# The last seven-product block's second group, product by product, with two token tiles normed and stored ahead of the others

## The chip, the cores and the metric

The kernel runs on one core of one Trainium2 chip. The metric is device microseconds for one execution. Names of engines as in the profile: PE is TensorE (PEld its weight loads), DVE is VectorE, ACT is ScalarE, POOL is GpSimd, SP is SyncE, which here issues DMAs.

## The reference

One layer of a decoder block over 512 tokens of width 2048. Cut to what the change touches:

```python
def _hybrid_layer(h, ...):
    u = _rmsnorm(h, norm_w)
    proj = jnp.matmul(u, w_in)                       # 2048 x 20528
    ...
    y_a = jnp.matmul(h_a, w_out[:ML_WIDTH])          # first 2048 rows of w_out
    y_b = jnp.matmul(h_b, w_out[ML_WIDTH:])          # last 2048 rows
    return jax.nn.sigmoid(gate_a) * y_a + jax.nn.sigmoid(gate_b) * y_b

def reference(x, ...):
    h = x + _hybrid_layer(x, ...)
    return _rmsnorm(h, final_norm_w)                 # over the 2048 columns of each token
```

All is float32. The change lies in the last step: the product `h_b` by the last 2048 rows of `w_out`, its gate, the sum with everything else, and the final norm.

## The kernel before, in words

**Precision.** Each float32 operand of a product is split into a high part (an ACT cast, `split_hi`, L135) and the rest (a DVE subtraction, `split_lo`, L138). One product of 128 rows by 512 columns is then three matmuls: high by high, rest by high, high by rest (L589 to L591).

**Token tiles.** The 512 tokens are four tiles of 128 (NC = 4): 0 and 1 are the lower half, 2 and 3 the upper.

**A seven-product block.** `seven_stage` (L499) computes 512 tokens by 1024 columns in blocks. Tokens, columns (`c1` and `c2`, NO = 512 each) and the 2048 rows of the weights are halved each, and eight half-size products become seven, at the price of sums of weights and of operands beforehand. A block has two groups, A with four products (m6, m1, m5, m7) and B with three (m1, m5, m7), each over KH = 8 "quads" of two 128-row weight tiles. For a quad, `load_quad` (L507) issues three 256 KB loads on SP into a buffer `wr3` (three of these); `prep_sums` and `prep_pair` make the weight sums on DVE (`t13`, `ts`) and split them. In group A, `ts` is w22 − w12 + w11 (of the four weight tiles w11, w12, w21, w22 by rows and columns): it is split, and also written to DRAM (`t2o_d`, on the ACT queue, L545), and group B reads it back and subtracts it from w21 (L549), which gives t4. Group B's products of a quad stand next to each other on PE: w21, w22, t4 with the operands `uh`/`ul` and `t4h`/`t4l`. The last six products of a block are in an order of their own (L610).

**The sums.** When a product has had its last quad, `ends` adds it up: U1 and C22 in the tile `X2`, m1 and m5 in PSUM (`add`, L637). In group B the sink takes over.

**The last stage.** OUTS has two blocks, columns 0 to 1023 and 1024 to 2047. Their sink is `sink_y` (L1328). It loads the gate tiles (`ty`, from `tg_d`, L1335, into the four 256 KB buffers tagged "wr") and multiplies: (gate + 1) by the sum (`put`, L1340). For the first block the result is added into `y_d` in DRAM by an accumulating DMA on POOL's queue (L1342). For the last block `y_d` has been loaded into the tile `hf`, 4 tiles by 2048 columns (`load_hf`, L1302, begun at the last block's group B by `open_hf`, L1320), the product is added to it on DVE (L1346), and ACT squares it with a running sum into `ssf` (L1347). The first 1024 columns are squared (L1316) and multiplied by the norm's weights `fw` on POOL (L1317) meanwhile.

**The end.** When all blocks are done, a loop over the four token tiles (L1441) makes each factor (a sum and a scale on DVE, a power on POOL), multiplies the first 1024 columns on ACT (L1446), the rest on DVE (L1449, L1452), and stores each half, 512 KB, on SP (L1447, L1453).

**What precedes.** The last 512-column block of the product by the first half of `w_out` is done plainly: 16 weight tiles, each for four token tiles, then four evictions on DVE (L1432), then the seven-product blocks begin. `h_sums` and the split of `h_b` (L1208, L1209) run beside it.

**Order.** PE's order is the program's. On the other engines a scheduler places instructions by priority: `tc.high_priority` and `urgent(n)` move them ahead, `behind(e)` puts one directly after the newest split on that engine. `start(generator, n)` runs a piece of side work n ticks later, a tick being about one product. Every engine and every DMA queue runs its own list in order: an instruction that waits holds those behind it.

Of the kernel before, what the change touches and what calls it, by code (L numbers as in the profile page):

```python
# [32 lines left out]
KLAST = 4  # L33
QWAIT = 9
# [21 lines left out]
def hybrid_body(  # L56
# [442 lines left out]
    def seven_stage(sbp, su, s4, X, t2_d, w_, k0, blocks, sinks, hook, by_half=False):  # L499
# [4 lines left out]
        quads = [(kind, c1, c2, b, g, i) for b, (kind, c1, c2) in enumerate(blocks) for g in "AB" for i in range(KH)]  # L504
        rawq, partq = [], {}
# [25 lines left out]
        def prep_sums(q):  # L531
# [5 lines left out]
            with tc.high_priority(offset=2 * PRIO):  # L537
                ts = wp.tile([P, 1, NO], F32, tag="tg", name="ts", bufs=3)
                if g == "A":
# [5 lines left out]
                    nc.scalar.dma_start(t2_d[b % 2, i], ts[:, 0, :])  # L545
# [30 lines left out]
        def seven(n0, kind, c1, c2):  # L576
# [4 lines left out]
                    "B": sinks[kind](c1, c2, m1, m5, m7, n0 + 2 * KH == len(quads))}  # L581

            def product(n, m, ts=range(2)):
# [3 lines left out]
                for t in ts:  # L587
# [7 lines left out]

            N = 2 * KH
            for n in range(N - 2):
                hook(n0 + n)
# [11 lines left out]
            for n, m in ((N - 2, 0), (N - 2, 1), (N - 1, 0), (N - 1, 1), (N - 2, 2), (N - 1, 2)):  # L610
# [5 lines left out]
                if last and m == 2 and by_half:  # L616

                    if n == N - 2:
                        for t in range(2):
                            product(N - 2, 2, (t,))  # L620
                            product(N - 1, 2, (t,))
                    continue
                if last and (n, m) == (N - 1, 1):
                    hook(len(quads) - 1)
# [118 lines left out]
    def begin_mixers(q):  # L743

        if q == 2 * KH * len(SEVEN) - 1:
            limit[0] = len(plan)
            prepare(nfront - 1)
# [511 lines left out]
    def close():  # L1259
        if "sb" not in late and not active:  # L1260
# [4 lines left out]
            late["ssf"] = sb.tile([P, NC, 3], F32, tag="ssf", name="ssf")  # L1265
            late["rf"] = sb.tile([P, NC], F32, tag="rf", name="rf")
# [30 lines left out]
    X2, ssf = late["X"], late["ssf"]  # L1297
    OUTS = [("y", c, c + NO) for c in range(0, D, 2 * NO)]
    hp = {}

    def load_hf():

        hf, fw = hp["hf"], hp["fw"]
        for i in range(4):
            nc.sync.dma_start(fw[:, i * NO:(i + 1) * NO], final_norm_w[i * NO:(i + 1) * NO].partition_broadcast(P))
            yield 1
        for c in (2, 3, 0, 1):
            nc.sync.dma_start(hf[:, c, HD:D], y_d[c, :, HD:D])
            yield 2
        for c in range(NC):  # L1310
            nc.sync.dma_start(hf[:, c, 0:HD], y_d[c, :, 0:HD])
            yield 2
        for c in range(NC):
            jk = hp["pool"].tile([P, HD], F32, tag="jk", name="jkf")
            with behind("A"):
                A.activation(jk, hf[:, c, 0:HD], AF.Square, accum_out=ssf[:, c, 0:1])  # L1316
            G.tensor_tensor(out=hf[:, c, 0:HD], in0=hf[:, c, 0:HD], in1=fw[:, 0:HD], op=ALU.mult)  # L1317
            yield 2

    def open_hf(q):  # L1320
        if q == 2 * KH * (len(OUTS) - 1) + KH:
            h2s.close()
            hp["pool"] = h2s.enter_context(tc.tile_pool(name="hfp", bufs=1))
            hp["hf"] = hp["pool"].tile([P, NC, D], F32, tag="hf", name="hf")
            hp["fw"] = hp["pool"].tile([P, D], F32, tag="fw", name="fw")
            start(load_hf(), 2)

    def sink_y(c1, c2, m1, m5, m7, last):  # L1328
# [8 lines left out]
        def put(key, ps, c, col, now=True):  # L1337
# [3 lines left out]
            if not last:  # L1341
                G.dma_start(y_d[c, :, col:col + NO], t, accum_op=ALU.add)  # L1342
                return
            o = hp["hf"][:, c, col:col + NO]
            with urgent(3) if now else behind("V"):
                V.tensor_tensor(out=o, in0=o, in1=t, op=ALU.add)  # L1346
            A.activation(t, o, AF.Square, accum_out=ssf[:, c, 1 + (col - c1) // NO:2 + (col - c1) // NO])  # L1347
# [6 lines left out]
        def half_b():  # L1354
# [5 lines left out]
            yield 2  # L1360
            if last:
                for t in range(2):
                    w = tgs[21, t] = hp["pool"].tile([P, NO], F32, tag=f"ty{t}", name="ty")
                    nc.sync.dma_start(w, tg_d[2 + t, :, D + c1:D + c1 + NO])
            yield 9 if last else 5
            for t in range(2):
                put((22, t), C22[t], 2 + t, c2, now=False)
                if last:
                    G.tensor_tensor(out=hp["hf"][:, 2 + t, c2:c2 + NO], in0=hp["hf"][:, 2 + t, c2:c2 + NO],
                                    in1=hp["fw"][:, c2:c2 + NO], op=ALU.mult)  # L1370
                yield 1
            yield 2 if last else 5
# [4 lines left out]
        def end7(t):  # L1377
            add(U1[t], U1[t], m7[t])
            if last:
                put((21, t), U1[t], 2 + t, c1)  # L1380
            else:
                start(late_((21, t), 2 + t, c1, U1[t]), 8 + 2 * t)
# [5 lines left out]
        start(half_b(), 4 * KH + 2)  # L1388
        return (lambda t: put((11, t), m1[t], t, c1)), end5, end7

    lead, seven = seven_stage(late["sb"], late["su"], late["s4"], X2, t2o_d, w_out, KT, OUTS, {"y": sink_y}, open_hf, True)
# [3 lines left out]
    for nb in range(YNARROW * NB // NO, D // NO):  # L1395
# [25 lines left out]
        for kt in range(KT):  # L1421
            hi, lo = next_w("o", nb * NO, kt)
# [61 lines left out]
```

## Time and profile before

| | us |
|---|---|
| median of three runs | 2243.85 (2242.92 to 2244.1) |
| profiled execution | 2241.4 |
| its span, first to last instruction | 2239.6 |
| mean granted clock | 0.993 |
| PE busy | 2174.5 (97%) |
| DVE, ACT, POOL busy | 1651.8, 944.0, 276.9 |

Times within the profile are in microseconds from the start of the span. A timeline row has the start, the length, the engine, the line, the operation, the tiles written and read, and in brackets how long the engine stood before it and what released it. A row of windows gives the length of a stretch and each engine's busy time in it. "SPq" and "POOLq" are instructions that issue DMAs.

### The profile page before, as it was taken

The numbers are of one execution on the slowest core, as the hardware profiler recorded it, in microseconds if no ns is written. First come the engines' busy times: TensorE is split into PE (matmuls) and PEld (weight loads), VectorE is DVE, ScalarE is ACT, GpSimd is POOL, SyncE is SP. The second block draws the span as 40 slices with busy tenths as digits, with TensorE's granted clock in tenths as the row PEclk, the third lists the DMA queues.
The fourth block names the chain that finished last, engine by engine and source line by source line (L and its number), as shares of the span: only waits on it lengthen the run. The fifth ranks groups of instructions, "written<-read, shape, count | busy, mean of one in ns | idle before, by whom it ended". The sixth has DMA issues, their size and how long they took to land.

```text
span 2239.6 us, 33118 instructions
## 1 busy us (share of the span) xinstructions
PE 2174.5 (97%) x11408; PEld 1817.6 (81%) x11408; DVE 1651.8 (74%) x2915; ACT 944.0 (42%) x1816; POOL 276.9 (12%) x342
## 2 busy tenths in 40 slices
PE   7999999999999999999999999999999999999995
PEld 5987878788778878887888888888888899987774
DVE  5787788788778777847877677776767774646786
ACT  4444444445444443443434344434434344333434
POOL 0320000000000000002322231313222110000003
PEclk9999999999999999999999999999999999999998
DMA  5456666667667766867676666667575566847686
GB/s 160 126 167 197 203 196 214 194 202 230 204 208 225 241 206 199 257 184 188 154 166 152 148 163 142 164 140 175 132 170 138 139 170 184 266 156 250 211 249 236
DMA packets 540203, 420.16 MB, mean 188 GB/s; under 512 B 241282, under 2 KB 417635, under 8 KB 540035
## 3 DMA queue, kind: packets, MB, share of 16 engines
q1 hardware_dynamic: 441986, 356.11, 56.7%
q10 hardware_dynamic: 96896, 59.86, 8.7%
q0 software_dynamic: 1152, 2.10, 0.6%
q8 instruction: 89, 1.46, 0.3%
q14 instruction: 80, 0.65, 0.1%
HBM read 332.93 MB, written 85.00 MB: 187 GB/s over the span
## 4 chain that ended last, share of the span: by engine, by line
PE 63%; DMA 16%; DVE 11%; issue 4%; SPq 3%; ACT 2%; POOL 0%; DVEq 0%; ACTq 0%; POOLq 0%
PE pj L257 9%; PE pj L259 9%; PE pj L258 9%; PE ps L590 8%; PE ps L589 8%; PE ps L591 8%; DVE wl L138 5%; DMA wr<-t_d 4%; DMA wr<-in_w_in_dram 3%; DMA wr<-t2o_d 2%; SPq L519 1%; PE pjt L272 1%; PE pjt L274 1%; PE pjt L275 1%; DMA hr<-h_d 1%
## 5 line engine op out<-in xcount | busy, mean ns | idle before, releaser
L135 ACT CAST wh<-wr 128x512 fp32r<-128x512 f32 (+1 forms) x560 | 390.1, 698 | 545.3 <-PE pj L258 290.0
L138 DVE TENSOR_TENSOR wl<-wr,wh 128x512 fp32r<-128x512 f32 (+1 forms) x560 | 462.9, 829 | 176.0 <-ACT wh L135 169.9
L257 PE MATMUL pj<-uh,wh 128*128 128x512 f32 x1024 | 429.6, 420 | 4.4 <-ACT yp L801 4.4
L259 PE MATMUL pj<-uh,wl 128*128 128x512 f32 x1024 | 401.4, 392 | 0.0
L258 PE MATMUL pj<-ul,wh 128*128 128x512 f32 x1024 | 400.4, 391 | 0.0
L589 PE MATMUL ps<-wh,uh 128*128 128x512 f32 x624 | 245.2, 393 | 8.1 <-DVE X L639 4.9
L590 PE MATMUL ps<-wl,uh 128*128 128x512 f32 x624 | 246.4, 395 | 5.0 <-DVE wl L138 4.7
L591 PE MATMUL ps<-wh,ul 128*128 128x512 f32 x624 | 243.6, 390 | 0.0
L259 PEld LDWEIGHTS pj<-uh,wl 128*128 128x128 f32 x1024 | 192.8, 188 | 43.3
L257 PEld LDWEIGHTS pj<-uh,wh 128*128 128x128 f32 x1024 | 193.8, 189 | 39.4 <-ACT yp L801 4.8
L135 ACT CAST wh<-ts 128x512 fp32r<-128x512 f32 x208 | 128.3, 617 | 228.2 <-DVE ts L549 180.2
L258 PEld LDWEIGHTS pj<-ul,wh 128*128 128x128 f32 x1024 | 193.8, 189 | 33.1
L135 ACT CAST wh<-t 128x1024 fp32r<-128x1024 f32 x104 | 109.5, 1053 | 232.9 <-PE ps L591 137.8
L590 PE MATMUL ps<-wl,suh 128*128 128x512 f32 x528 | 205.6, 389 | 0.5 <-DVE wl L138 0.5
L589 PE MATMUL ps<-wh,suh 128*128 128x512 f32 x528 | 205.7, 390 | 0.3 <-ACT to L650 0.2
L591 PE MATMUL ps<-wh,sul 128*128 128x512 f32 x528 | 205.4, 389 | 0.0
L138 DVE TENSOR_TENSOR wl<-ts,wh 128x512 fp32r<-128x512 f32 x208 | 144.9, 700 | 31.5 <-ACT wh L135 31.5
L138 DVE TENSOR_TENSOR wl<-t,wh 128x1024 fp32r<-128x1024 f32 x104 | 127.3, 1224 | 45.8 <-ACT wh L135 45.3
L589 PEld LDWEIGHTS ps<-wh,uh 128*128 128x128 f32 x624 | 117.1, 188 | 39.9 <-DVE X L639 12.0
L590 PEld LDWEIGHTS ps<-wl,uh 128*128 128x128 f32 x624 | 117.1, 188 | 38.2 <-DVE wl L138 15.3
L272 PE MATMUL pjt<-wh,uh 128*128 128x256 f32 x512 | 147.4, 288 | 0.7 <-ACT tgs L757 0.7
L274 PE MATMUL pjt<-wl,uh 128*128 128x256 f32 x512 | 144.7, 283 | 0.0
(307 smaller groups left out, 3812.9 us busy)
## 6 DMA issues: line engine op xcount, KB each, us to landing
wr<-in_w_in_dram SPq DMA_DIRECT2D x680, 256.0 KB, 3.7
wr<-in_w_out_dram SPq DMA_DIRECT2D x144, 256.0 KB, 4.5
t_d<-ts ACTq DMA_DIRECT2D x88, 256.0 KB, 4.4
wr<-t_d SPq DMA_DIRECT2D x88, 256.0 KB, 4.0
wr<-in_w_in_dram SPq DMA_DIRECT2D x96, 128.0 KB, 3.1
xt<-in_x_dram SPq DMA_DIRECT2D x8, 512.0 KB, 7.9
v<-v_d SPq DMA_DIRECT2D x8, 512.0 KB, 6.2
gb<-rows_d SPq DMA_DIRECT2D x16, 256.0 KB, 5.0
```

What stands on the lines that cost most here:

```text
L135: newest["A"] = A.copy(hi, src).ins
L138: newest["V"] = V.tensor_tensor(out=lo, in0=src, in1=hi.bitcast(F32), op=ALU.subtract).ins
L257: T.matmul(ps[j], hi[:, k, wsl], uh[:, kt, :], start=(kt == 0), stop=False)
L258: T.matmul(ps[j], hi[:, k, wsl], ul[:, kt, :], start=False, stop=False)
L259: T.matmul(ps[j], lo[:, k, wsl], uh[:, kt, :], start=False, stop=(kt == KT - 1))
L272: T.matmul(o, uh[:, kt, tsl], hi[:, k, :], start=(kt == 0 and c % 2 == 0), stop=False, skip_group_check=True)
L274: T.matmul(o, uh[:, kt, tsl], lo[:, k, :], start=False, stop=False, skip_group_check=True)
L275: T.matmul(o, ul[:, kt, tsl], hi[:, k, :], start=False, stop=(kt == KT - 1), skip_group_check=True)
L519: nc.sync.dma_start(r[:, n, :], src[n])
L589: T.matmul(ps[t], ah, hi, start=(g == "A" and i == 0), stop=False, skip_group_check=True)
L590: T.matmul(ps[t], ah, lo, start=False, stop=False, skip_group_check=True)
L591: T.matmul(ps[t], al, hi, start=False, stop=(i == KH - 1), skip_group_check=True)
```

## The change

In the last of the two output blocks:

- **Group A.** For each quad a further tile `b21` (w21, 256 KB) is loaded on SP into a "wr" buffer. POOL subtracts `ts` from it, which gives t4, and its own queue stores t4 where `ts` went before (`t2o_d`). The ACT queue's store is gone there.
- **Group B** no longer goes quad by quad but product by product: eight pieces of m5 (w22), eight of m7 (t4, read back ready), eight of m1 (w21). A piece is one 256 KB load on SP into a "wr" buffer, one cast, one split, and the six matmuls of the product's two token tiles. Loads run four pieces ahead, splits two to three.
- **Side work** is given by hand, piece by piece, in the table `beside`: loads of `y_d` in twelve parts, of the weights in two, the gate products, sums and squares. Additions for `c2` and six multiplications by weights are on POOL.
- **The last four pieces** (KLAST) are done for token tile 0 first, then for 1. Ahead of them in the program stand the factor products and the stores of tiles 2 and 3, whose sums are complete after m7.
- All eight gate tiles are loaded late in group A, into the `wr3` buffers.

Elsewhere:

- **KTAIL.** In the last plain block, the last two weight tiles are done token tile by token tile, with each tile's eviction directly behind it. The evictions of both plain 512-column blocks are at `urgent(3)` instead of `urgent()`.
- **Addresses.** `ssf` and `rf`, 64 bytes a partition together, move from the pool `sb2` into the tile `bia`. The tiles `t13` and `w2h`, `w2l` (and the operands `tuh`, `tul`) begin at a multiple of 512 bytes in a partition thereby; they began 96 bytes past one.
- The hooks `open_hf` and `begin_mixers` are simplified and `by_half` is gone.

```diff
+                    if in_final(b):
+                        G.tensor_tensor(out=b21[q], in0=b21[q], in1=ts[:, 0, :], op=ALU.subtract)
+                        G.dma_start(t2_d[b % 2, i], b21[q])
+                        load_b21(q + 1)
+                    else:
+                        nc.scalar.dma_start(t2_d[b % 2, i], ts[:, 0, :])
...
+                b21[q] = wp.tile([P, NO], F32, tag="wr", name="b21", bufs=NRAW)
+                nc.sync.dma_start(b21[q], w_[k2, c1:c1 + NO])
...
+                for m in range(4):
+                    for n in (KH - 2, KH - 1):
+                        fin(2 * m + n - KH + 2)
+                        product(n, m)
+                fin(8)
+                return
...
-            late["ssf"] = sb.tile([P, NC, 3], F32, tag="ssf", name="ssf")
-            late["rf"] = sb.tile([P, NC], F32, tag="rf", name="rf")
...
+    ssf, rf = bia[:, 0:3 * NC].rearrange("p (c n) -> p c n", c=NC), bia[:, 3 * NC:4 * NC]
...
+    def final_y(c1, c2, m1, m5, m7, lhs, split, t4_d):
...
+        pieces = [(m, i) for m in (1, 2, 0) for i in range(KH)]
...
+        def load_gates():
+            order = ((2, c2), (3, c2), (0, c2), (1, c2), (2, c1), (3, c1), (0, c1), (1, c1))
+            for n, (c, col) in enumerate(order):
+                if n % 3 == 0:
+                    t = late["sb"].tile([P, 3, NO], F32, tag="wr3", name="ty", bufs=3)
+                o = ty[c, col] = t[:, n % 3, :]
+                nc.sync.dma_start(o, tg_d[c, :, D + col:D + col + NO])
+                yield 1
+        def load():
+            if len(rawp) < len(pieces):
+                m, i = pieces[len(rawp)]
+                k2 = slice((KT + 2 * i + 1) * P, (KT + 2 * i + 2) * P)
+                with tc.high_priority(offset=2 * PRIO):
+                    r = wp.tile([P, 1, NO], F32, tag="wr", name="wr", bufs=NRAW)
+                    newest["S"] = nc.sync.dma_start(r[:, 0, :], (w_out[k2, c1:c1 + NO], w_out[k2, c2:c2 + NO], t4_d[i])[m]).ins
+                rawp.append(r)
+        def prep():
+            if len(partp) < len(pieces):
+                with tc.high_priority(offset=2 * PRIO):
+                    partp.append(split(rawp[len(partp)], False)[0])
...
+        beside = {
+            0: [lambda: known(2, c2, D)], 1: [lambda: known(3, c2, D)], 2: [lambda: known(0, c2, D)],
+            3: [lambda: known(1, c2, D), lambda: times(2, c2, C22[0])],
+            4: [lambda: known(2, c1, c2), lambda: times(3, c2, C22[1]), lambda: plus(2, c2, G)],
+            5: [lambda: known(3, c1, c2), lambda: plus(3, c2, G)],
+            6: [lambda: weight(0, HD), lambda: square(2, c2, D, 2)],
+            7: [lambda: square(3, c2, D, 2)],
+            8: [lambda: known(2, 0, HD), lambda: add(m5[0], U1[0], m5[0])],
+            9: [lambda: add(m5[1], U1[1], m5[1]), lambda: times(0, c2, m5[0])],
+            10: [lambda: known(3, 0, HD), lambda: times(1, c2, m5[1]), lambda: plus(0, c2, G)],
+            11: [lambda: plus(1, c2, G), lambda: square(2, 0, HD, 0), lambda: weigh(2, 0, HD)],
+            12: [lambda: weight(HD, D)],
+            13: [lambda: square(3, 0, HD, 0), lambda: weigh(3, 0, HD), lambda: known(0, 0, HD)],
+            14: [lambda: square(0, c2, D, 2)],
+            15: [lambda: square(1, c2, D, 2), lambda: weigh(0, c2, D), lambda: known(1, 0, HD)],
+            16: [lambda: weigh(1, c2, D), lambda: add(U1[0], U1[0], m7[0]), lambda: times(2, c1, U1[0], False), lambda: plus(2, c1, V, False),
+                 lambda: square(2, c1, c2, 1), lambda: known(0, c1, c2), lambda: known(1, c1, c2)],
+            17: [lambda: add(U1[1], U1[1], m7[1]), lambda: times(3, c1, U1[1], False), lambda: plus(3, c1, V, False),
+                 lambda: square(3, c1, c2, 1), lambda: factor(2), lambda: square(0, 0, HD, 0), lambda: weigh(0, 0, HD)],
+            18: [lambda: factor(3), lambda: square(1, 0, HD, 0), lambda: weigh(1, 0, HD)],
+        }
...
+            for t in range(2):
+                for j in range(len(pieces) - KLAST, len(pieces)):
+                    if t == 0 and j < len(pieces) - KLAST + 2:
+                        c = 2 + j - len(pieces) + KLAST
+                        by_act(c, 0, HD)
+                        store(c, 0, HD)
+                        by_dve(c, HD, D)
+                        store(c, HD, D)
+                    part(j, t)
+                times(t, c1, m1[t], False)
+                plus(t, c1, V, False)
+                square(t, c1, c2, 1, False)
+                factor(t, False)
+                by_act(t, 0, HD, False)
+                store(t, 0, HD)
+                by_dve(t, c1, c2, False)
+                by_dve(t, c2, D, False, True)
+                store(t, HD, D)
...
+        tail = KTAIL if nb == D // NO - 1 else 0
...
+        ws = [next_w("o", nb * NO, kt) for kt in range(KT - tail, KT)]
         for c in range(NC):
-            with urgent():
+            for i, w in enumerate(ws):
+                products(KT - tail + i, c, *w)
+                if i % 2:
+                    tick()
+            with urgent(3):
                 V.scalar_tensor_tensor(out=tgs[c], in0=tgs[c], scalar=1.0, in1=ps[c], op0=ALU.add, op1=ALU.mult)
```

Of the helpers in it, `known` loads a part of `y_d` into `hf` and `weight` a part of `fw`; `times` is the gate product on DVE, `plus` the addition into `hf`, `square` ACT's square with its sum, `weigh` the product with `fw` on POOL, `factor` the reduction, scale and power, `by_act` and `by_dve` the two halves of the last product, `store` the output DMA. Those not marked `False` are issued right behind the newest split of their engine.

More of the change, by code (lines that the diff above doesn't have):

```diff
@@ L33 @@
 KLAST = 4
+KTAIL = 2
 QWAIT = 9
@@ L615, in seven @@
                     load_quad()
[L616 to L622, printed above, removed]
                 if last and (n, m) == (N - 1, 1):
-                    hook(len(quads) - 1)
+                    hook()
                 product(n, m)
@@ L1296, in hybrid_body @@
     t2o_d = dr.tile([2, KH, P, NO], F32, tag="t2o", name="t2o_d")
-    X2, ssf = late["X"], late["ssf"]
+    X2 = late["X"]
     OUTS = [("y", c, c + NO) for c in range(0, D, 2 * NO)]
[L1299 to L1326, printed above, removed]
+    ssf, rf = bia[:, 0:3 * NC].rearrange("p (c n) -> p c n", c=NC), bia[:, 3 * NC:4 * NC]
     def sink_y(c1, c2, m1, m5, m7, last):
@@ L1340, in put @@
                 V.scalar_tensor_tensor(out=t, in0=t, scalar=1.0, in1=ps, op0=ALU.add, op1=ALU.mult)
[L1341 to L1347, printed above, removed]
+            G.dma_start(y_d[c, :, col:col + NO], t, accum_op=ALU.add)
         def late_(n, c, col, x_):
@@ L1378, in end7 @@
             add(U1[t], U1[t], m7[t])
[L1379 to L1382, printed above, removed]
+            start(late_((21, t), 2 + t, c1, U1[t]), 8 + 2 * t)
         def end5(t):
@@ L1437, in hybrid_body @@
         seven(2 * KH * b, *blk)
[L1438 to L1453 removed]
+    assert not active
 def hybrid_block(tc, *args):
```

167 lines of the change are left out of this document (121 added, 46 removed).

## The prediction

> **What bounds the kernel now.** I read the page's whole-span figures first, then busy time by five-microsecond windows over the end, then the timeline there.
>
> ```profile
> PE 2174.5 (97%) x11408; PEld 1817.6 (81%) x11408; DVE 1651.8 (74%) x2915; ACT 944.0 (42%) x1816; POOL 276.9 (12%) x342
> ```
> ```profile
> 2130.00:2180.00 50.00, 49.24 (x212) 39.15 (x210) 41.31 (x53) 18.11 (x26) 5.19 (x6) 1.00 0.87 247
> ```
> ```profile
> 2190.00:2195.00 5.00, 5.00 (x23) 4.00 (x23) 1.76 (x3) 1.61 (x2) 0.00 (x0) 1.00 1.05 395
> ...
> 2210.00:2215.00 5.00, 5.00 (x23) 4.04 (x23) 5.00 (x4) 2.53 (x6) 5.00 (x3) 1.00 0.00 0
> ```
>
> In each window row the busy times of PE, PEld, DVE, ACT and POOL follow its length; the last three figures are the clock, the DMA share and GB/s. TensorE is the bound for 97% of the span. In the last block's first group (row 2130:2180) VectorE is busy 41.3 of 50 us, so it has 8.7 to spare. In the second group the DMA engines are full (395 GB/s at 2190), then empty (0 at 2210). The output leaves when all else is over:
>
> ```profile
> 2215.15 0.39 PE L591 MATMUL ps<-wh,ul 128*128 128x512 f32 x1
> ...
> 2224.57 0.61 ACT L1347 ACTIVATE ty<-hf 128x512 f32<-128x512 f32 x1
> ...
> 2224.78 3.55 POOL L1445 TENSOR_TENSOR rf<-rf,mhalf 128x1 f32<-128x1 f32 x4 [4.71 <-DVE rf L1443]
> 2225.09 0.19 ACT L1347 ACTIVATION_READ_ACCUMULATOR ty<-hf 128x1 f32 x1
> 2225.31 0.16 DVE L1442 TENSOR_REDUCE rf<-ssf 128x1 f32<-128x3 f32 x1 [0.27 <-ACT ty L1347]
> 2225.39 4.27 ACT L1446 ACTIVATE hf<-hf,rf 128x1024 f32<-128x1024 f32 x4
> ...
> 2226.56 0.34 SPq L1447 DMA_DIRECT2D out_dram<-hf  x1
> ...
> 2233.28 1.19 SPq L1453 DMA_DIRECT2D out_dram<-hf  x1
> ```
> ```profile
> wr<-in_w_out_dram SPq DMA_DIRECT2D x30, 256.0 KB, 5.8
> hf<-y_d SPq DMA_DIRECT2D x8, 512.0 KB, 7.6
> out_dram<-hf SPq DMA_DIRECT2D x8, 512.0 KB, 4.9
> ...
> y_d<-ty POOLq DMA_DIRECT2D x6, 256.0 KB, 7.4
> ```
>
> The last matmul ends at about 2215.4 (its row starts at 2215.15 and is drawn 0.39 long; starts are 0.23 apart). The span ends at 2239.6. So 24.2 us are tail: eight stores of 512 KB from 2226.56 to 2233.28, the last landing 4.9 us after its issue is over.
>
> **The tail: minus 13.** The two upper token tiles (2 and 3) have their factors and stores before the last pieces end. Behind the last matmul only tile 1 is left: gate product, addition (0.68 each, as the 128x512 VectorE rows below), square and its read (0.61 and 0.19), reduce (0.16) and scale (as much, two instructions of 128x1), power (3.55/4 = 0.89), ScalarE product (4.27/4 = 1.07), issue (0.34 alone, 1.19 when queued), landing 4.9. The sum is 9.7 to 10.5; tile 0's two stores share the wire with tile 1's, so I take 11. Tail 24.2 − 11 = 13.2 gained; 12 to 14.5 as ends.
>
> **Group B by pieces: plus 5.5.** Eight quads of three loads and three products become 24 pieces of one 256 KB load and one product each, in the order m5, m7, m1; a piece is 6 matmuls, 6 × 0.23 = 1.38 us. The eight sums t4 leave VectorE here. Each needs one cast, one residual split and one load, and both rings (raw, split) hold four. A buffer's round is landing + cast 0.61 (as a 128x512 ScalarE row) + split 0.68; four pieces of PE are 5.5 us. So a landing of 4.2 us is free, and each microsecond above it costs one per round, some five rounds in 24 pieces after the ring's first filling.
>
> ```profile
> hf<-y_d SPq DMA_DIRECT2D x3, 512.0 KB, 7.4
> wr<-in_w_out_dram SPq DMA_DIRECT2D x4, 256.0 KB, 7.1
> ```
> ```profile
> DMA packets 2659, 4.85 MB, mean 243 GB/s; under 512 B 297, under 2 KB 297, under 8 KB 2658
> ...
> wr<-in_w_out_dram SPq DMA_DIRECT2D x8, 256.0 KB, 4.7
> ```
>
> The first fence is window 2180 to 2190 (350 GB/s), the second 2160 to 2180. At 243 GB/s a piece lands in 4.7; beside a flood of hf loads in 7.1. Group B keeps its bytes: 24 pieces (6.3 MB), hf (8 × 512 KB = 4.2 MB), weights 1.0 MB: 11.5 MB over 33 us is 348 GB/s, but hf now comes one load every one to three pieces instead of in a flood. I take 4.9: five rounds of 0.7 are 3.5. Ends: 4.4 (+1) and 6.5 (+11.5).
>
> ```profile
> 2194.43 0.95 SPq L519 DMA_DIRECT2D wr<-in_w_out_dram  x2
> ```
>
> SP issues 24 pieces, 12 hf loads (8 before) and two of weights (4 before) in this stretch: 38 × 0.48 = 18 us of 33, so its queue holds, as long as no load at its head waits.
>
> ```profile
> 2207.02 0.68 DVE L138 TENSOR_TENSOR wl<-ts,wh 128x512 fp32r<-128x512 f32 x1
> ...
> 2209.36 2.90 DVE L138 TENSOR_TENSOR wl<-ts,wh 128x512 fp32r<-128x512 f32 x1
> 2212.19 1.27 DVE L1340 SCALAR_TENSOR_TENSOR ty<-ty,ps 128x512 f32<-128x512 f32 x2
> ```
> ```profile
> 2202.17 2.54 POOL L1369 TENSOR_TENSOR hf<-hf,fw 128x512 f32<-128x512 f32 x2 [45.11 <-DMA wr<-in_w_out_dram]
> 2208.74 11.33 POOL L1317 TENSOR_TENSOR hf<-hf,fw 128x1024 f32<-128x1024 f32 x4 [4.04 <-ACT jkf L1316]
> ```
>
> The same split takes 0.68 and, begun while GpSimd multiplies hf by the weights (11.33/4 = 2.83 each), 2.90: it waits until GpSimd's instruction ends. Before, those four fell where no split was due; now four of 2.83 and six of 1.27 (two weight products, four additions) lie between pieces 4 and 18, beside splits on which the next load depends. One hit costs up to 2.2 us; the split ring runs up to two pieces ahead, 2.8 us, while landings are on time. I add 2 (ends 0 and 5).
>
> By the Trainium skill's "SBUF — State Buffer" (Who interferes with whom), the loser of the shared port blocks for the whole instruction of whoever issued first; the trace agrees (2.90 against 0.68). What that would make of the time is the third rival.
>
> **Group A with t4 computed on GpSimd: plus 6.** Eight GpSimd subtractions (1.27 each), eight GpSimd-queue stores in place of eight ScalarE ones, and eight more 256 KB loads, which take their buffers from the four "wr" that the ty tiles use.
>
> ```profile
> PE ps L590 <- DVE wl L138: 1.6, 4, 0.6
> PE ps L589 <- DVE X L639: 0.8, 1, 0.8
> ```
> ```profile
> 2126.25 0.69 DVE L543 TENSOR_TENSOR ts<-wr,t 128x512 f32<-128x512 f32 x1
> ...
> 2135.66 0.68 DVE L1340 SCALAR_TENSOR_TENSOR ty<-ty,ps 128x512 f32<-128x512 f32 x1
> ...
> 2136.63 0.86 POOL L1342 DMA_DIRECT2D y_d<-ty  x1 [0.94 <-DVE ty L1340]
> ...
> 2138.61 5.25 SPq L1335 DMA_DIRECT2D ty<-tg_d  x4
> ```
> ```profile
> 2143.95 14.29 SPq L519 DMA_DIRECT2D wr<-in_w_out_dram  x12
> ```
>
> The fourth ty tile of the block before now takes the buffer of the first t4. That one is free only when its subtraction (behind the ts of quad 0 that ends at 2126.94, plus 1.27) and its store have landed: 0.86 of issue, then 4.9 (the out row) to 7.4 (the y_d row), so 2134 to 2136.5; then the ty load, 4.9 more: 2139 to 2141. The gate product that ran at 2135.66 waits for it. Queued behind it on VectorE are the U1 sum and quad A1's splits, for which TensorE waits from about 2137.5: 1.5 to 3.5, I take 2.5. SP stands likewise before the 2138.61 group, whose later tiles need the y_d landings, so that the quads' loads of 2143.95 slip 3 to 4; the three-deep ring leaves 1 of it at quad 4 and 2.5 at quad 7. Together 6 (ends 2 and 10). VectorE's spare 8.7 covers eight port hits of up to 1.27; without it they cost up to 10.
>
> Before's own waits in this block are 2.4 by the waits view (1.6 + 0.8), some 3.2 from start to start, since the matmul ahead of a wait is drawn with its length. They go: the 0.8 for X because group B now begins with m5, which reads no sum, the 1.6 because the new waits above take their place. So minus 3.2.
>
> **KTAIL: minus 1.5.**
>
> ```profile
> 2051.28 0.40 PE L591 MATMUL ps<-wh,tul 128*128 128x512 f32 x1
> ...
> 2053.60 0.68 DVE L1432 SCALAR_TENSOR_TENSOR X<-X,py 128x512 f32<-128x512 f32 x1
> ...
> 2054.43 0.47 PE L589 MATMUL ps<-wh,uh 128*128 128x512 f32 x1 [2.75 <-DVE X L1432]
> ```
> ```profile
> 2055.00:2059.00 4.00, 4.00 (x12) 3.15 (x11) 4.00 (x7) 0.69 (x2) 0.00 (x0) 0.57 0.82 285
> ```
>
> TensorE stands 2.75 for the eviction at 2053.60, and runs four microseconds at clock 0.57, which costs 4 × 0.43 = 1.7. The eviction of tile 0 may now start 4 us sooner, but stays behind the same splits on VectorE, and the last weight tile's split is needed some 1.5 earlier. Between 0 and 4.5 I take 1.5.
>
> "TensorE: Matmul & The Clock Gate" (Part 1: The HAM clock gate) in the Trainium skill has the clock halve after some 3.4 us of idle; the trace shows it after 2.75 with short gaps before. By either, a group-A wait of 3.5 would cost 1.7 more, and my 2.5 none.
>
> **Operands at 512 bytes: minus 2.**
>
> ```profile
> L589 PE MATMUL ps<-wh,suh x240: 389/389/499, 518.2 to 874.0; 128*128 128x512 f32 x120
> ```
> ```profile
> L589 PE MATMUL ps<-wh,tuh x90: 387/394/400, 2060.2 to 2178.2; 128*128 128x512 f32 x90
> ```
>
> The accumulators ssf and rf, moved out of the pool, take the 96 bytes out of the addresses behind them; the move itself issues nothing, and the two removed hooks and the by-half order cost nothing either, being done while the program is written. The same matmul has a median of 389 ns in the first stage and 394 in the last two blocks. If placing is all of it, 672 matmuls × 5 ns are 3.4; DMA load differs too, so 0 is the other end and 2 my value.
>
> **The sum.** −13.2 + 5.5 + 6 − 3.2 − 1.5 − 2 = −8.4 us. The profiled execution took 2241.4 (span 2239.6 and 1.8 around it), 2.45 below the median; the difference goes on the median: 2243.85 − 8.4 = 2235.5. One part in 500, 4.5 us, is about what separates a change from none here.
>
> **The rivals.**
>
> *The waits stay hidden* (22%): t4's store lands early, pieces in 4.4; A costs 2 and B 1. Sum −16.9: 2227. For it: the DMA engines stood empty from 2210 to the first store at 2226.56, which is now used. Against: the buffer chain above is a hard dependence.
>
> *The last tiles are not alone in the tail* (11%): GpSimd's row of work from piece 10 on (two additions, four weighings, two halves, two powers: 18.2 us by the rows above) ends after the matmuls; the powers of tiles 0 and 1 queue behind it, and the upper stores (1.19 each) come late. Costs 5: 2240.5, the same. Against: pieces 10 to 23 last 19.3.
>
> *Pieces land slowly* (11% slower, 10% the same): the four raw buffers of group B.
>
> ```profile
> wr<-in_w_out_dram SPq DMA_DIRECT2D x4, 256.0 KB, 8.3
> ```
>
> This is window 2190 to 2205, at 397 GB/s. A landing of 6.2 costs 5 × 2 = 10, thus −1.9 (2242). From 6.6 on the change loses; at 7.1 it costs 14.5, thus +2.6; at 8.3 it costs 20.5, thus +8.6; with a half clock beside it I put this case at 2251. For it: 348 GB/s is the load of the 7.1 row. Against: 4.7 at 243, and hf loads spread out.
>
> *Every GpSimd pass stops a split* (4%, slower): 4 × 2.83 + 6 × 1.27 = 19 us, less the 2 already in the sum: +8.6, 2252. For it: the one split that met a weighing took 2.90. Against: the next two VectorE instructions (2212.19) read PSUM and took 1.27 together beside the same GpSimd work, and a pass that starts behind the split costs it nothing. The Trainium skill's "SBUF — State Buffer" (Who interferes with whom), cited above, has this as its rule.
>
> **Numbers.** Forecast 42% (2231 to 2239). The chances add up to one: faster by over 4.5 us with the forecast and the hidden waits, 0.64; the same with the shared tail and a middling landing, 0.21; slower 0.15. The range 2225 to 2246 takes in the first rival and the middling landing, and leaves out the slower cases and a little at each edge.
>
> **What would show it.** Last matmul to end near 11 (tail step); first group-A wait of about 2.5 at some 2137 behind ty's gate product, and POOL's store ahead of that ty load; pieces' landing 4.7 to 5.2 with splits of 2 us or more beside POOL's weighings; no 0.57 window behind 2051; medians of 389 in the last two blocks. A landing over 6, or a tail over 15, makes the prediction wrong.

## The result, and the profile after

The changed kernel takes 2255.45 us, median of five runs (2251.02 to 2256.77); the kernel before 2243.85 (2242.92 to 2244.29). The ratio is 1.0049, with a 95% interval of 1.0035 to 1.0064: slower by 11.6 us where 8.4 less were forecast, and outside the range.

Read from the starts of their first matmuls, the stages of the two profiled executions stand like this (us):

| stage | before | changed | difference |
|---|---|---|---|
| from the span's start to the last plain block | 2005.4 | 2009.3 | +3.9 |
| the last plain block (16 weight tiles, 192 matmuls) | 44.7 | 46.2 | +1.5 |
| first output block, group A | 48.8 | 44.5 | −4.4 |
| first output block, group B | 34.6 | 37.3 | +2.7 |
| last block, group A | 45.3 | 58.3 | +13.0 |
| last block, group B, first two thirds (pieces 0 to 15) | 24.5 | 21.9 | −2.5 |
| last block, group B, last third (pieces 16 to 23) | 11.8 | 23.8 | +12.0 |
| last matmul's start to the end (the tail) | 24.4 | 11.4 | −13.0 |

In the kernel before, the rows of group B stand for the first 96 and the last 48 of its matmuls. Up to the first row's end the two kernels run the same instructions, and only the priority of one block's evictions differs. In the fourteen profiled executions of this study that point lies between 2003.0 and 2012.3, so the 3.9 is not put down to the change; the other rows add up to about 9. Stages are compared by their lengths, and kernels by their medians. Two of the expectations below speak of the plain block's last four weight tiles; the lengths that they give (44.7, 46.2, 47.5) are those of all 16.

Busy time of the changed kernel by stage (length, then PE, PEld, DVE, ACT and POOL, clock, DMA share, GB/s): group A, pieces 0 to 15, pieces 16 to 23, tail.

```profile
2137.23:2195.56 58.33, 49.77 (x193) 39.12 (x192) 45.27 (x51) 18.19 (x27) 17.32 (x19) 0.88 0.83 241
2195.56:2217.47 21.91, 21.91 (x98) 17.95 (x96) 16.17 (x21) 11.45 (x21) 8.37 (x5) 1.00 0.88 301
2217.47:2241.50 24.03, 16.58 (x49) 11.06 (x47) 20.49 (x22) 11.73 (x23) 13.85 (x8) 0.79 0.54 198
2241.50:2252.60 11.10, 0.12 (x1) 0.00 (x0) 4.03 (x10) 3.02 (x4) 1.27 (x2) 0.73 0.51 208
```

The first 16 pieces run without a gap: 21.91 us of TensorE in 21.91. The last eight have 16.58 in 24.03, with VectorE busy for 20.49 and a clock of 0.79. What TensorE waited for in the changed kernel's last block, by releaser (us in total, times, longest):

```profile
PE ps L1414 <- DVE wl L139: 6.1, 4, 2.0
PE ps L610 <- DVE ty L1342: 5.1, 1, 5.1
PE ps L611 <- DVE wl L139: 2.2, 2, 1.4
PE ps L610 <- ACT wh L136: 2.0, 1, 2.0
PE ps L1414 <- DVE bia L1448: 1.4, 1, 1.4
```

**The tail** is what was forecast: the last matmul starts at 2241.23, the span ends at 2252.6, and only two tiles are stored after it.

**Group A's gate product.** The changed kernel's timeline, where the buffer chain of the prediction runs:

```profile
2130.83 2.15 POOL L560 TENSOR_TENSOR b<-b,ts 128x512 f32<-128x512 f32 x1 [12.84 <-DMA wr<-in_w_out_dram]
...
2133.28 0.61 POOL L561 DMA_DIRECT2D t2o_d<-b  x1 [0.30 <-POOL b L560]
...
2137.81 0.33 SPq L1337 DMA_DIRECT2D ty<-tg_d  x1
...
2145.20 0.69 DVE L1342 SCALAR_TENSOR_TENSOR ty<-ty,ps 128x512 f32<-128x512 f32 x1 [4.61 <-DMA ty<-tg_d]
```
```profile
2140.41 0.39 PE L612 MATMUL ps<-wh,tul 128*128 128x512 f32 x1
2145.94 0.80 PE L610 MATMUL ps<-wh,tuh 128*128 128x512 f32 x1 [5.15 <-DVE ty L1342]
2146.54 0.63 PE L611 MATMUL ps<-wl,tuh 128*128 128x512 f32 x1
2146.97 0.63 PE L612 MATMUL ps<-wh,tul 128*128 128x512 f32 x1
```

Subtraction (itself stretched from 1.27 to 2.15), store, gate load, gate product, TensorE: every link is there. The load landed 7.1 us after its issue was over (2138.14 to 2145.20) where 4.9 was reckoned, and TensorE stood 5.15. Behind it, and again behind the waits ahead of the last quad, some ten matmuls start 0.43 apart instead of 0.23; these 20 cost group A 4 us more.

**Group B's splits.** Two stretches of the changed kernel's timeline, at the splits of pieces 15 to 18 and of 21 and 22:

```profile
2215.46 6.29 DVE L139 TENSOR_TENSOR wl<-wr,wh 128x512 fp32r<-128x512 f32 x3 [1.10 <-ACT wh L136]
2215.47 9.19 POOL L1442 TENSOR_TENSOR hf<-hf,fw 128x1024 f32<-128x1024 f32 x4
...
2222.86 0.68 DVE L1420 SCALAR_TENSOR_TENSOR ty<-ty,X 128x512 f32<-128x512 f32 x1
2223.47 1.75 DVE L139 TENSOR_TENSOR wl<-wr,wh 128x512 fp32r<-128x512 f32 x1
```
```profile
2229.69 5.15 POOL L1442 TENSOR_TENSOR hf<-hf,fw 128x1024 f32<-128x1024 f32 x2 [0.57 <-ACT jkf L1431]
2230.16 2.45 DVE L139 TENSOR_TENSOR wl<-wr,wh 128x512 fp32r<-128x512 f32 x1 [1.68 <-ACT wh L136]
...
2232.60 2.78 DVE L139 TENSOR_TENSOR wl<-wr,wh 128x512 fp32r<-128x512 f32 x1
```

Three splits in a row take 6.29 together where 0.68 is the length of one alone, then 1.75, 2.45 and 2.78, each beside GpSimd's weight products. Five of the eight splits of pieces 16 to 23 are stretched so, and each of the five ends 0.54 to 0.56 us after one of the weight products does. TensorE waits 6.1 us for splits here. The landings, which the prediction had feared, are a little shorter than it reckoned; issue to landing of the pieces of m7 and m1:

```profile
wr<-t2o_d SPq DMA_DIRECT2D x8, 256.0 KB, 4.6
...
wr<-in_w_out_dram SPq DMA_DIRECT2D x8, 256.0 KB, 4.1
```

They set the pace all the same. The casts of pieces 9, 10, 12 and 14 to 17 begin 0.1 us after their tile has landed, and the lead of a piece's cast over its first matmul shrinks from 3.4 us at piece 9 to 1.2 at piece 15. So the first 16 pieces lost no time on TensorE, but little was left in hand when the weight products began.

### The profile page after: what moved, and what is told of

It is laid out like the page before. It is cut to its first block, busy times and chain, and to the rows that moved or that the text cites. A ratio compares the mean times of both kernels' runs of the same rounds, so it can differ in the third digit from the quotient of the medians.

```text
span 2252.6 us, 33199 instructions
## 1 busy us (share of the span) xinstructions
PE 2183.0 (97%) x11408; PEld 1822.1 (81%) x11408; DVE 1658.0 (74%) x2911; ACT 944.6 (42%) x1824; POOL 294.0 (13%) x362
## 5 line engine op out<-in xcount | busy, mean ns | idle before, releaser
L136 ACT CAST wh<-wr 128x512 fp32r<-128x512 f32 (+1 forms) x576 | 396.2, 690 | 554.1 <-PE pj L259 275.3
L139 DVE TENSOR_TENSOR wl<-wr,wh 128x512 fp32r<-128x512 f32 (+1 forms) x576 | 479.9, 836 | 178.7 <-ACT wh L136 168.6
L611 PE MATMUL ps<-wl,uh 128*128 128x512 f32 x592 | 234.0, 395 | 6.5 <-DVE wl L139 6.4
L610 PE MATMUL ps<-wh,uh 128*128 128x512 f32 x592 | 232.8, 393 | 6.0 <-DVE X L670 5.6
L612 PE MATMUL ps<-wh,ul 128*128 128x512 f32 x592 | 231.1, 390 | 0.0
L136 ACT CAST wh<-ts 128x512 fp32r<-128x512 f32 x200 | 123.4, 617 | 222.1 <-DVE ts L568 180.5
L139 DVE TENSOR_TENSOR wl<-t,wh 128x1024 fp32r<-128x1024 f32 x104 | 132.0, 1269 | 42.7 <-ACT wh L136 42.0
L139 DVE TENSOR_TENSOR wl<-ts,wh 128x512 fp32r<-128x512 f32 x200 | 139.1, 699 | 31.3 <-ACT wh L136 31.3
L276 PE MATMUL pjt<-wh,ul 128*128 128x256 f32 x512 | 144.8, 283 | 0.0
L611 PEld LDWEIGHTS ps<-wl,uh 128*128 128x128 f32 x592 | 111.4, 188 | 38.7 <-DVE wl L139 17.0
```

The lines of the kernel that those rows point to most:

```text
L136: newest["A"] = A.copy(hi, src).ins
L139: newest["V"] = V.tensor_tensor(out=lo, in0=src, in1=hi.bitcast(F32), op=ALU.subtract).ins
L276: T.matmul(o, ul[:, kt, tsl], hi[:, k, :], start=False, stop=(kt == KT - 1), skip_group_check=True)
L610: T.matmul(ps[t], ah, hi, start=(g == "A" and i == 0), stop=False, skip_group_check=True)
L611: T.matmul(ps[t], ah, lo, start=False, stop=False, skip_group_check=True)
L612: T.matmul(ps[t], al, hi, start=False, stop=(i == KH - 1), skip_group_check=True)
```

## The experiments

Two theories for the lost time: **port**, that GpSimd's passes over SBUF stop VectorE's splits, in both groups; and **landing**, that pieces come too late for four buffers. For group A also the **buffer chain** and the w21 loads. All lengths below are stages as in the table above; for the last third of group B the measure is 8 x 1.37 = 11.0 us without a wait (1.37 is a sixteenth of the 21.91 above).

### GpSimd's weight products left out

```diff
         def weigh(c, a, b):
-            G.tensor_tensor(out=hf[0][:, c, a:b], in0=hf[0][:, c, a:b], in1=fw[0][:, a:b], op=ALU.mult)
+            pass
```

> The changed kernel without the six GpSimd products of hf by the norm's weights (its output is not the normed one: columns 0 to 1023 of all tiles and 1536 to 2047 of tiles 0 and 1 lack their weights). All else stays, loads too. Theory 'port': GpSimd's passes stop the residual splits, so pieces 16 to 23 fall from 23.8 us to about 12, the half-clock stretches there go, and the time falls by 11 to 13. Rival 'landing': pieces land too late for four raw buffers; then pieces 16 to 23 stay over 20 and the time falls by 3 at most. Group A stays at 58 either way.

One execution: 2243.08. Pieces 16 to 23 take 16.2 (7.6 less), group A 58.3 as in the changed kernel. No split of pieces 17 to 23 is stretched any more (min/median/max in ns):

```profile
L139 DVE TENSOR_TENSOR wl<-wr,wh x7: 682/692/693, 2213.8 to 2225.2; 128x512 fp32r<-128x512 f32 x7
```

So most of the loss at the end of group B goes with these six instructions, though their loads stayed. But 5.2 above 11.0 remain where about 1 was expected, and in these the landing theory has a part. The pieces loaded at 2212 to 2217.5 land later than those of the changed kernel:

```profile
wr<-in_w_out_dram SPq DMA_DIRECT2D x4, 256.0 KB, 5.7
```

The cast of piece 20 begins at 2219.35, 0.1 after its tile has landed, and TensorE soon waits 1.61 for the cast of piece 21. That piece's tile lands at 2221.57, and its cast stands behind three squares on ScalarE until 2222.43. Landing falls as the main cause, not as a part.

### The same work on GpSimd, in parts of 256 columns

```diff
+            for k in range(a, b, NB):
+                G.tensor_tensor(out=hf[0][:, c, k:k + NB], in0=hf[0][:, c, k:k + NB], in1=fw[0][:, k:k + NB], op=ALU.mult)
```

and the GpSimd additions likewise.

> The changed kernel with GpSimd's weight products and additions of group B in parts of 256 columns, same work. Theory 'port': VectorE is let in between parts, so no split takes more than about 1.4 us instead of 2.8, pieces 16 to 23 take 14 to 16 us instead of 23.8 and the time falls by 7 to 10. Rival 'landing': no change (within 2 us).

Median 2247.21 of ten runs, 8.2 below the changed kernel; ratio to the kernel before 1.0017 (1.0003 to 1.0030). The splits of pieces 9 to 23, by line and tile (min/median/max in ns), in the changed kernel and here:

```profile
L139 DVE TENSOR_TENSOR wl<-wr,wh x15: 674/692/2784, 2205.1 to 2235.4; 128x512 fp32r<-128x512 f32 x15
```
```profile
L139 DVE TENSOR_TENSOR wl<-wr,wh x15: 677/865/1225, 2197.0 to 2223.7; 128x512 fp32r<-128x512 f32 x15
```

The longest split falls from 2.78 to 1.23, as a wait for one GpSimd instruction would have it, and no matmul of pieces 16 to 23 is at half clock any more. Pieces 16 to 23 take 18.7, 5.1 less (14 to 16 were expected): more splits are touched, each for less. The tail grows to 14.2, since GpSimd gets to its powers later.

### Group A: the subtraction on VectorE

```diff
-                        G.tensor_tensor(out=b21[q], in0=b21[q], in1=ts[:, 0, :], op=ALU.subtract)
-                        G.dma_start(t2_d[b % 2, i], b21[q])
+                        V.tensor_tensor(out=b21[q], in0=b21[q], in1=ts[:, 0, :], op=ALU.subtract)
+                        nc.scalar.dma_start(t2_d[b % 2, i], b21[q])
```

> The changed kernel with group A's t4 subtraction on VectorE and its store on ACT's queue; buffers as they are. Theory 'port' for group A: the 128x1024 splits return from 2.0 to 1.22 us, the wait ahead of the last quad (4.4 us) goes, group A falls from 58.3 to about 53; the 5.5 us wait for the gate product stays, since its buffer chain stays. Rival 'VectorE is full': with 0.69 more for each quad on VectorE the last quad's wait stays at 3 or more, and group A stays at 57 or more.

Median 2245.82 of ten (ratio 1.0016, 1.0002 to 1.0030); group A 52.2. The 128x1024 splits of group A, in the changed kernel and here (count, busy us, mean ns):

```profile
L139 DVE TENSOR_TENSOR wl<-t,wh 128x1024 fp32r<-128x1024 f32 x7 | 13.4, 1916 | 2.6 <-ACT wh L136 2.6
```
```profile
L139 DVE TENSOR_TENSOR wl<-t,wh 128x1024 fp32r<-128x1024 f32 x7 | 8.5, 1219 | 0.5 <-ACT wh L136 0.5
```

VectorE does eight subtractions more (0.69 each) and still gains, since each GpSimd subtraction had cost it 0.7 on one split. The last quad's wait falls from 4.5 to 1.9, start to start; the gate product's wait stays, as expected (3.8 in the waits view). Theory "port" holds for group A too, and "VectorE is full" falls. The store moved from GpSimd's queue to ScalarE's in the same edit; what that gave by itself was not tried.

### Group A: the first w21 tile later

```diff
-                if n == N - 3 and n0 + N + 1 < len(quads) and in_final(quads[n0 + N][3]):
-                    load_b21(n0 + N)
...
                     if in_final(b):
+                        if q not in b21:
+                            load_b21(q)
```

> The changed kernel with the first w21 tile of group A asked for after the gate tiles (12,0) and (12,1) of the block before, so that neither waits for a t4 store. Theory 'buffer chain': the 5.5 us wait for the gate product and the half clock behind it go, group A falls from 58.3 to about 51 and the time by about 6. Rival 'the wait moves': the w21 load then stands in SP's queue for a gate tile's accumulation, the quads behind it come late, and group A keeps 56 or more.

Median 2249.14 of ten (ratio 1.0024, 1.0011 to 1.0037). The rival was right: TensorE's waits in the last block are now

```profile
PE ps L613 <- DVE wl L139: 5.9, 4, 3.5
...
PE ps L612 <- ACT wh L136: 1.7, 1, 1.7
```

with none for the gate product, and group A takes 55.9. The w21 loads stand at the head of SP's queue for the gate tiles' accumulations (9.5 us in 2110 to 2150), and the quads' loads behind them. But group B of the *first* block, which nothing in the prediction touched, returns from 37.3 to 34.4. In the changed kernel the first w21 load had stood 3.2 us in SP's queue there. Its SP waits in 2110 to 2150:

```profile
SPq L519 <- DMA y_d<-ty: 10.1, 4, 3.9
...
SPq L1337 <- DMA t2o_d<-b: 2.2, 1, 2.2
```

That this load is what cost the 3 us is not shown. Six later kernels do not have it there either, and the stage takes 34.8 to 38.2 in them, one execution each.

### Both groups mended, apart and together

Group A: w21 tiles only for quads 3 to 7, subtraction on VectorE; quads 0 to 2 store ts, and group B subtracts. Group B: no GpSimd weight products, VectorE multiplies by factor and weights at the end; in `beside` the loads and squares of columns 0 to 1023 also come earlier, and the two upper additions of m7's columns go to GpSimd.

```diff
+                    if in_final(b) and i >= NLATE:          # NLATE = 3
+                        V.tensor_tensor(out=b21[q], in0=b21[q], in1=ts[:, 0, :], op=ALU.subtract)
+                        nc.scalar.dma_start(t2_d[b % 2, i], b21[q])
...
+                    if j in wx:                             # group B, m7 pieces 0 to 2
+                        V.tensor_tensor(out=r[:, 0, :], in0=wx[j], in1=r[:, 0, :], op=ALU.subtract)
```
```diff
-                by_act(t, 0, HD, False)
+                by_dve(t, 0, HD, False)
                 store(t, 0, HD)
-                by_dve(t, c1, c2, False)
-                by_dve(t, c2, D, False, True)
+                by_dve(t, HD, D, False)
```

> The changed kernel with another group A: t4 only for quads 3 to 7, on VectorE and stored from ACT's queue, so that no w21 tile stands among the block's early gate tiles; quads 0 to 2 store ts as before, and group B loads w21 beside it for three of its pieces. Theory 'buffer chain and port': both waits of group A go, it takes 46 to 49 us instead of 58.3 (52.2 with the VectorE subtraction alone), the stalls at the end of the first output block go with them (37.3 to about 34.5), group B and tail as in the changed kernel, the time 10 to 13 lower than its 2255. Rival 'VectorE is full': group A stays over 51.

> The changed kernel with another group B: no GpSimd weight products (VectorE multiplies by factor and weights in one pass at the end), loads and squares of columns 0 to 1023 earlier, the two upper additions of m7's columns on GpSimd. Theory 'port': pieces 16 to 23 take 11.5 to 14 us instead of 23.8, the half clock there goes, the tail grows from 11.4 by 0 to 1.5, the time falls by 9 to 12. Rival 'ACT's squares and VectorE's own work also hold the splits back': pieces 16 to 23 stay at 16 or more, as without weighings (16.2).

> Both mended groups together. If the causes are separate, the gains add: group A 46 to 49, pieces 0 to 23 in 34 to 37, tail 11.5 to 13, time about 2255 less 20 to 23, thus 2232 to 2235, and faster than the kernel before by 8 to 12. If one wait merely hides another, less than 15 of the 20 come.

| | group A | pieces 0 to 15 | 16 to 23 | tail | median of ten | ratio to before |
|---|---|---|---|---|---|---|
| changed | 58.3 | 21.9 | 23.8 | 11.4 | 2255.45 (five) | 1.0049 |
| A mended | 48.3 | 25.9 | 22.7 | 12.3 | 2246.54 | 1.0011 (0.9996 to 1.0026) |
| B mended | 57.4 | 21.9 | 15.6 | 14.1 | 2245.82 | 1.0018 (1.0004 to 1.0031) |
| both | 50.5 | 25.8 | 17.0 | 15.0 | 2240.43 | 0.9995 (0.9983 to 1.0007) |

The two causes are mostly separate: by the medians 8.9 and 9.6 alone and 15.0 together, where 20 to 23 were expected, and each stage keeps most of its gain in the kernel with both. That kernel cannot be told from the kernel before. With group B mended, pieces 16 to 23 lie between the 11.5 to 14 of the theory and the 16 of its rival. The first block's group B was expected near 34.5 with A mended and took 36.8. Against expectation the tail grows by up to 3.6 (VectorE's last products, 1.22 each, now stand ahead of tile 0's gate product), and with A mended pieces 8 to 15 by 3.4, where three of the m7 pieces need two loads each.

### Plain block and operands alone

The kernel before with KTAIL and with `ssf` and `rf` in `bia`.

> The kernel before with only the last plain block token tile by token tile and with the accumulators out of the pool. Predicted -3.5: the median matmul of the last two blocks falls from 231 to 227 ns from start to start (672 of them: -2.7), the 2.75 us wait and the half clock behind it go (first block's group A 48.8 to 44), while the last four weight tiles of the plain block take 1.5 to 4 longer (44.7 to 46.2 or more). Rival: the wait is only moved ahead, and the two stretches together stay at 93.5 less 0.8.

Median 2240.55 of ten, ratio 0.9991 (0.9974 to 1.0007): by the time alone no difference is shown. The matmuls of the last two blocks here, against the 387/394/400 of the prediction:

```profile
L590 PE MATMUL ps<-wh,tuh x96: 388/389/397, 2056.5 to 2181.0; 128*128 128x512 f32 x96
```

Start to start the median goes from 231 to 227 ns: 672 x 4 = 2.7 us. No run moves the addresses alone, but the edit to the plain block is over before these matmuls begin. The last plain block and the first group A together take 47.8 + 43.5 = 91.3 instead of 93.6; 0.8 of the 2.3 is operands by this count (192 matmuls), and the other 1.5 is put down to the plain block. In the twelve profiled executions with two tiles done token tile by token tile this sum lies between 90.1 and 92.8. The wait did not go: it is now ahead,

```profile
2047.33 0.50 PE L1423 MATMUL py<-wh,uh 128*128 128x512 f32 x1 [0.35 <-ACT wh L136]
2048.22 0.50 PE L1424 MATMUL py<-wl,uh 128*128 128x512 f32 x1 [0.38 <-DVE wl L139]
2048.55 0.40 PE L1425 MATMUL py<-wh,ul 128*128 128x512 f32 x1
2049.80 0.61 PE L1423 MATMUL py<-wh,uh 128*128 128x512 f32 x1 [0.85 <-ACT wh L136]
```

where the last weight tiles' splits are needed sooner, and only shorter.

### Weights on VectorE; one tile less; no w21 in group A

Three kernels on the ground of both mends. The first takes the products of columns 0 to 1023 by the weights, GpSimd's in the change, to VectorE between pieces 12 and 19:

```diff
-            G.tensor_tensor(out=hf[0][:, c, a:b], in0=hf[0][:, c, a:b], in1=fw[0][:, a:b], op=ALU.mult)
+            with behind("V"):
+                V.tensor_tensor(out=hf[0][:, c, a:b], in0=hf[0][:, c, a:b], in1=fw[0][:, a:b], op=ALU.mult)
```

the second has KTAIL = 1 besides, the third NLATE = 8.

> Both mended groups, and the products of columns 0 to 1023 by the weights on VectorE between pieces 12 and 19 instead of in the last pass, so that ScalarE takes the last product of those columns again. The same work as in the changed kernel's GpSimd products, on the engine that GpSimd stopped: if the port is what cost, pieces 8 to 23 stay at 31 us or less (31.2 with both mended groups, 34.8 in the changed kernel) though VectorE does 4 x 1.22 us more, and the tail falls from 15.0 to about 11.5. Time 3 to 4 below that of both mended groups (2240.4): 2236.5, faster than the kernel before by 5 to 8. Rival 'any work beside the splits costs': pieces 8 to 23 take 34 or more, and nothing is gained.

> The kernel of weigh_dve with one weight tile instead of two done token tile by token tile. The stretch of the plain block's last four weight tiles returns from about 47.5 to 45 to 46, the first wait of the seven-product blocks comes back in part (group A of the first block 43.5 to 44.5 or 46). Net within 1.5 us of weigh_dve either way.

> The kernel of weigh_dve with no t4 in group A at all: ts is stored as before for all quads, and group B loads w21 beside ts for all eight m7 pieces and subtracts on VectorE. Group A returns to 45.3 to 47 (46.5 with only operands and plain block changed), which shows the rest of its loss to be the w21 tiles; pieces 8 to 15 rise from 14.3 to 16 to 19, as eight subtractions and two loads a piece stand there. Net -1 to +2 against weigh_dve.

The first: median 2239.22 of twelve against 2244.4 beside it, ratio 0.9981 (0.9969 to 0.9993): faster than both kernels, by less than the 5 to 8 expected. Pieces 8 to 23 take 30.2 with the weights on the very engine that does the splits, the tail 13.2. The second: 2240.7; the last plain block 45.7, but first group A 48.2, so that the two stretches together are 93.9 against 91.9 with two tiles. The third: 2245.05; group A 46.9, so the w21 tiles were the rest of its loss, but pieces 8 to 15 take 25.3 where 16 to 19 were expected. There VectorE waits for loads at last:

```profile
DVE wr L1412 <- DMA wx<-in_w_out_dram: 7.0, 4, 3.5
```

With two loads a piece, landing costs more than it did with one.

### The second tiles earlier

The kernel of the faster one, with the three w21 tiles of group B loaded at pieces 1 to 3, m7's two upper additions on VectorE, and the last weight product behind the last split.

```diff
+                if j in (1, 2, 3):
+                    load_wx(KH + j - 1)
```

> The kernel of weigh_dve with three things moved: the three w21 tiles that group B's first m7 pieces need are loaded 4 to 5 pieces earlier, into the three ts buffers that group A has left; the two upper additions of m7's columns are on VectorE instead of GpSimd; the last weight product stands behind the last split. Theory: what is left of group B's waits is the late second tile of these pieces (3.5 us in pieces 8 to 15) and the port and VectorE's row at pieces 20 to 23 (3.1), so pieces 8 to 15 fall from 14.5 to about 12, 20 to 23 from 8.4 to 6 or 7, and the time from 2239.2 to 2235. Rival: the bandwidth at the start of group B is what is short; then pieces 0 to 7 get slower by what 8 to 15 gain.

Median 2240.95 of twelve, ratio 0.9995 (0.9984 to 1.0007). The two waits went as expected (pieces 8 to 15 take 12.7, 20 to 23 take 6.6), and the rival came too: the new loads go out with the eight gate tiles while group A ends, five of the first piece loads are issued only from 2179.07 on, and TensorE stands 3.8 us between the groups; pieces 0 to 7 take 13.7 instead of 11.4. Nothing is gained over the kernel it is made from.

## Why the prediction was wrong

**Tail, −13.2: right.** 24.4 to 11.4 from the last matmul's start, and 11 was the forecast.

**Pieces landing, +3.5: not told apart.** They landed in 4.1 to 4.6, not 4.9, and the first 16 pieces lost nothing but used up their lead. In the last third 5.2 us stayed without the weight products, with landings of 5.7 as a part of it. The rival "pieces land slowly" (21% in its two halves, 6.2 or more) did not come.

**Port hits in group B, +2 with 0 to 5 as ends: the step that failed.** Pieces 16 to 23 lost 12.8, of which 7.6 went with the weight products. I had the row (2.90 against 0.68), the list of ten GpSimd passes and the Trainium skill's rule, and gave the case in which they count 4%. Two reasons put against it do not hold. That the next two VectorE instructions read PSUM is true of them and not of splits, which read two SBUF tiles. That "a pass that starts behind the split costs it nothing" did not help, because GpSimd's work is back to back (four passes in 9.19 us), and five of these eight splits ran beside one. Leaving the products out gave 7.6 back, doing them on VectorE or at the end 8.0 to 8.2; what a split loses also delays the next cast and the next load into that buffer. Besides, 17 matmuls of these pieces start 0.43 apart behind waits of about 2 us, 3.4 us of the 12.8. By the Trainium skill's "SBUF — State Buffer" (Who interferes with whom) the second to issue blocks until the first has finished; the runs agree (at most 2.78 beside whole passes, at most 1.23 beside passes of 256 columns).

**Group A, +6 with 2 to 10 as ends: the mechanism right, the size not.** The chain was named link by link, and its wait came at 2140; 2.5 became 5.3 start to start, since a stretched subtraction and a landing of 7.1 add up. The last quad lost 4.5, not 2.5, and not by SP's slip alone: "VectorE's spare 8.7 covers eight port hits" failed. Seven long splits took 13.4 instead of 8.5, and with each quad near 5.7 us on VectorE (45.27 in eight quads) there was no spare to make good the first wait. The subtraction on VectorE brought 6.2 back. And half clock took 4.0, which the sum had at none.

**First block's group B: missed.** I followed SP's queue only from the last block on, and the first w21 load stands in it one group earlier. The stage lost 2.7; whether because of this load stays open.

**Before's waits, −3.2; KTAIL, −1.5; operands, −2:** the waits did go; KTAIL comes to −1.5 by the difference above, from one execution each; operands to −2.7.

So the gains came about as reckoned, and the rival with 4% came in kind, in both groups at once. That its 2252 lies near the measured 2255 is partly luck: it counted 19 us of stops in group B, where the last third lost 12.8 and the first 16 pieces, with additions on GpSimd beside them, none; and it left group A at 6, which lost 13.

## What to carry to other kernels

In this kernel work moved to GpSimd was not moved off VectorE, because the splits and GpSimd's passes both read SBUF. Reckon each GpSimd pass as a possible stop of its full length for the VectorE instruction beside it, and look at whether that instruction feeds the bound engine through a short ring. Before extra tiles go into a shared ring of buffers, follow who waits for each buffer and, in every in-order queue, what stands behind that load. A rival for which the profile already shows one full-sized instance deserves more than a few per cent.

## What the runs showed of the hardware

The clock halved after shorter waits than the 2.75 us of the kernel before. In the changed kernel's last pieces:

```profile
2230.18 0.49 PE L1413 MATMUL ps<-wh,uh 128*128 128x512 f32 x1
2232.67 0.54 PE L1414 MATMUL ps<-wl,uh 128*128 128x512 f32 x1 [1.99 <-DVE wl L139]
2233.01 0.63 PE L1415 MATMUL ps<-wh,ul 128*128 128x512 f32 x1
```

A wait of 1.99 us, four matmuls after a run at half clock, was enough; "TensorE: Matmul & The Clock Gate" in the Trainium skill (Part 1: The HAM clock gate) has some 3.4 us of idle for it, which fits the 5.15 us wait of group A but not this row of waits. What rule holds for waits in a row was not tried.

The same instructions up to some 2000 us brought the fourteen executions to the last plain block at 2003.0 to 2012.3. A single time of this kernel can therefore not show an effect of a few microseconds; the lengths of stages could.
